# The pooled branch's products as one sum of three 256-column passes, and a later place for two weight loads

## The chip, the cores and the metric

The kernel runs on one core of a Trainium2 chip. The metric is the device time of one execution in microseconds; less is better. A core has a matmul engine (TensorE, PE in the profile, its weight loads PEld), VectorE (DVE), ScalarE (ACT), GpSimd (POOL) and SyncE (SP), whose queue issues nearly all DMA transfers here. Each engine runs its own instructions in order and waits on the others by semaphores. Matmuls read SBUF and write PSUM, which has eight banks of 128 x 512 float32; four of them (`mmp`, tag `mm`) serve the sums that this change is about.

## What is computed

An encoder trunk of two layers over 256 tokens of 1024 channels, in float32. A layer has a token mixer (a pooled branch, an attention branch, gates and an output projection) and a gated MLP with a convolution of width 3. Of the reference, cut to the pooled branch and the MLP:

```python
pooled = jnp.stack([_centred_mean(ug[:, :, gi], w) for gi, w in enumerate(POOL_WINDOWS)], axis=2) - ug
pool_out = jnp.einsum('bsgc,gcd->bsgd', pooled, w_pool).reshape(B, S, POOL_WIDTH) * pool_scale
...
merged = jax.nn.sigmoid(g_pool) * (pool_out @ w_a) + jax.nn.sigmoid(g_attn) * (attn_out @ w_b)
...
a, gval = jnp.split(xn @ w_up, 2, axis=-1)
a = lax.conv_general_dilated(a, conv_w[:, None, :], ...) + conv_b
return (jax.nn.gelu(a) * gval) @ w_down
```

There are four pooled groups of 256 channels each, so `w_pool` has four products of 256 tokens by 256 channels by 256 channels in a layer.

## The kernel before

**Two parts for every operand.** TensorE works on a 32-bit type with fewer mantissa bits than float32. Every weight and every activation is therefore split into a high part, rounded to that type, and a rest: `wh` and `wl`, `x2[..., 0]` and `x2[..., 1]`. A product is the sum of high by high, high by rest and rest by high. The split of a weight piece (128 x 1024 numbers) is one ScalarE copy (L252) and one VectorE subtraction (L254).

**The stream of weights.** The class `Weights` holds two lists that are written down before the kernel starts: `loads` (transfers of 1 MB from memory into a raw tile, issued on SP's queue by L171) and `pieces` (halves of a load, or slices, in the order in which TensorE uses them). `W.get()` hands out the next piece and makes sure that the three or four behind it are being split. A raw tile is one of three (`RAW`); the next load waits until both of its pieces are split. A split piece is one of five (`BUFS`); ScalarE waits until TensorE has left it. Loads leave in the order in which they were added. A load with a tag of its own (`ybig`, `at2`) goes into another tile and doesn't count among the three.

**The mixer and the pooled branch.** The input projection runs in groups (`GROUPS`) of 512 columns; each is four steps of 12 matmuls (L753, tile `t_ps`, 512 columns each). Between the steps of the last two groups, q1 and k1, stand the pooled branch's products, one of the four groups behind every second step: `visits` lists which generator is advanced behind which step. `pool_out` works a group off in two stages that are separated by a `yield`, so that the second stage is issued one step later. A group has two chunks of 128 output channels. For a chunk, `two_sums` multiplies the high weight by both parts of the pooled values at once (512 columns), and the weight's rest by the high part (256 columns, into the second half of the bank). ScalarE then scales the second half (L1166), VectorE scales the first and adds (L1169); one step later ScalarE rounds the result to `po2`'s high part (L1175) and VectorE subtracts it (L1178). `po2` is used from the second half of the next projection on.

**The MLP.** `MLP_GROUPS` sets the order: g0, a1, g1, a2, g2 (groups of the up projection, 512 columns in four steps; a0 ran before), then `("w", 3)`, a block that makes two further groups out of seven products of quadrants of the weight instead of eight, with steps of the down projection (tile `res_ps`, L670 to L672) between them. The block's products are L1582. Two of its quadrants, "11" and "12", are loaded by `first_quadrants` into the tiles tagged `ybig` and `at2` ahead of the block, because their differences (L343) are weights as well. When a group's sums are complete, VectorE transposes them (L807), one transfer of 0.5 MB sends them to memory (L812, tile `crossing`), and four transfers bring them back with channels on the partitions (L819, tiles `zga` and `zg`). All of these share SP's queue with the loads.

Of the kernel before, what the change touches and what calls it, by code (L numbers as in the profile page):

```python
# [289 lines left out]
def encoder(ctx, tc, x, w_in, w_pool, pool_scale, w_a, w_b, w_o, norm1, norm2, w_up, conv_w,  # L290
            conv_b, w_down, rel_bias, norm_f, onehot, edges, out):
    nc = tc.nc
# [71 lines left out]
    for l in range(DEPTH):  # L364
        for g in range(NG):
            c0 = C_V + g * 512
            slots = (("m2", 0, 2), ("m2", 1, 2), ("ybig",), ("at2",)) if g == 0 else ()
            for j in range(2):
                tag = "k1" if l == 0 and g == 1 and j == 0 else None
                W.use(rows(w_in[l], j * 512, 4, c0, 512, tag), slots[2 * j : 2 * j + 2])  # L370
        if l == 0:
            W.n_scaled = len(W.pieces)
        for kind, n in GROUPS:
            c0 = {"u": 0, "q": C_Q, "k": C_K}[kind] + n * 512
            pieces = rows(w_in[l], 0, 4, c0, 512)
# [84 lines left out]
    hps = const.tile([P, DEPTH, 8], F32, name="hps")  # L460
# [178 lines left out]
            nc.sync.dma_start(out=ov[:, t, middle], in_=xn[:, middle])  # L639
            yield  # L640

    turns = {"rest": False}

    def two_sums(x2, nk, *chunks):

        wide, rests = ([(c, k, kind) for c in chunks for k in range(nk)] for kind in (True, False))
        first = rests if turns["rest"] else wide
        last = wide if turns["rest"] else rests
        for steps in (first, last):
            for (ps, wh, wl), k, kind in steps:
                out, w, x = (ps, wh, x2[:, k]) if kind else (ps[:, 1], wl, x2[:, k, 0])
                nc.tensor.matmul(  # L657
                    out, w(k), x, start=(steps is first and k == 0),
                    stop=(steps is last and k == nk - 1), skip_group_check=turns["rest"],
                )  # L660
        turns["rest"] = not turns["rest"]

    def halves(a):

        return a.rearrange("p (t m) -> p t m", t=2)
# [360 lines left out]
    for l in range(DEPTH):  # L1026
# [21 lines left out]
        if l == 0:  # L1048
            with tc.manual_schedule():
                begun = begin_values_of_x()  # L1050
                W.by_hand = 1
                x2 = first_values(*begun, keep_values)
                W.by_hand = 0
        else:
            for g in range(NG):
                held = begun[0] if g == 0 else [W.get() for _ in range(4)]
                for t in range(2):
                    if g + t == 0:
                        ps = begun[1]
                    else:  # L1060
                        ps = v_tile()
# [34 lines left out]
        us, pooled, got = {}, {}, {}  # L1096
# [50 lines left out]
        def pool_out():  # L1147
            for j in (1, 0):
                if j:
                    po2 = got["po2"] = two_parts("m2", "po2")  # L1150
                i, (wh, wl) = W.get()
                for gg in range(2):
                    ps = [mmp.tile([P, 2, S], F32, tag="mm", name="pool_ps") for _ in range(2)]
                    for oc in range(2):
                        cc = slice(oc * P, (oc + 1) * P)
                        two_sums(
                            pooled[2 * j + gg], 2,
                            (ps[oc], lambda k: wh[:, 2 * gg + k, cc], lambda k: wl[:, 2 * gg + k, cc]),
                        )
                    if gg:  # L1160
                        W.free(i)
                    po = [sm.tile([P, 2, P], F32, tag="u", name="po") for _ in range(2)]
                    first = 4 * j + 2 * gg
                    for oc in range(2):
                        sc = hps[:, l, first + oc : first + oc + 1]
                        nc.scalar.mul(out=po[oc], in_=halves(ps[oc][:, 1]), mul=sc)  # L1166
                    for oc in range(2):
                        sc = hps[:, l, first + oc : first + oc + 1]
                        nc.vector.scalar_tensor_tensor(  # L1169
                            out=po[oc], in0=halves(ps[oc][:, 0]), scalar=sc, in1=po[oc],  # L1170
                            op0=ALU.mult, op1=ALU.add,
                        )
                    yield
                    for oc in range(2):
                        nc.scalar.copy(out=po2[:, first + oc, 0], in_=po[oc])  # L1175
                    for oc in range(2):
                        c = first + oc
                        nc.vector.tensor_sub(out=po2[:, c, 1], in0=po[oc], in1=po2[:, c, 0].bitcast(F32))  # L1178
                    yield

        first_parts = {}
# [119 lines left out]
        def keep_gated(n):  # L1301
# [36 lines left out]
        with tc.manual_schedule():  # L1338
            W.by_hand = 1
            for kind, n in GROUPS:  # L1340
                ps = None
                for i in range(4):
                    ps = by_tokens(x2, 4, ps=ps, begin=i, end=i + 1)
# [6 lines left out]
            po2 = got["po2"]  # L1350
# [15 lines left out]
            first = None  # L1366
# [314 lines left out]
```

## Time and profile before

| | us |
|---|---|
| median of 3 runs | 850.63 |
| lowest, highest | 850.13, 852.48 |
| the profiled execution | 851.33 |
| its span, from the first instruction to the last | 849.5 |
| TensorE busy | 840.6 |
| VectorE busy | 645.6 |
| ScalarE busy | 523.8 |

The profile is of one execution. Its span is what the views show; the 1.8 us between the span and the execution's time lie before and behind. Matmuls overlap in the pipeline, so a matmul's duration (0.39 us for 512 columns) is longer than its share of the time: what counts is the step from one start to the next. A row of the timeline has start, duration, engine, line, operation, tiles, shapes and count, and in brackets how long the engine had been idle and what ended it.

### The profile page before, as it was taken

What the parts mean: (1) busy time and instruction counts of PE and PEld (TensorE: products, weight loads), DVE (VectorE), ACT (ScalarE), POOL (GpSimd) and SP (SyncE); (2) the same over time, 40 slices, a digit from 0 to 9 for tenths busy, and PEclk for the clock granted to TensorE, in tenths of its full rate; (3) what the DMA queues carried; (4) which work ended last, traced back from release to release, by engine and by line L of the source; (5) the groups of instructions that cost most, each with busy time, mean ns of one, the idle gap of its engine ahead of it and who ended that gap; (6) DMA issues with size and microseconds to landing.
All of it is one profiled execution on the core that took longest, in us unless ns stands there. A gap on an engine that the chain in (4) does not pass through costs nothing.

```text
span 849.5 us, 10951 instructions
## 1 busy us (share of the span) xinstructions
PE 840.6 (99%) x3901; PEld 700.9 (83%) x3901; DVE 645.6 (76%) x838; ACT 523.8 (62%) x757; POOL 34.0 (4%) x96
## 2 busy tenths in 40 slices
PE   9999999999999999999999999999999999999997
PEld 7888888888888878888888888888888888888886
DVE  6968777757767699898665686878567878998874
ACT  7744566654554776688645454677455658757883
POOL 1610000000010000000000000000000100000000
PEclk9999999999999999999999999999999999999999
DMA  8699897785759885898735889868777499769861
GB/s 303 213 307 294 302 292 242 260 276 210 251 191 299 278 266 198 264 328 294 232 120 200 261 275 313 279 206 271 252 250 278 152 332 296 246 205 289 305 198 51
DMA packets 147968, 214.03 MB, mean 252 GB/s; under 512 B 7801, under 2 KB 69185, under 8 KB 147913
## 3 DMA queue, kind: packets, MB, share of 16 engines
q1 hardware_dynamic: 147480, 212.67, 75.9%
q10 hardware_dynamic: 432, 0.66, 0.2%
q8 instruction: 31, 0.51, 0.2%
q14 instruction: 25, 0.20, 0.1%
HBM read 186.02 MB, written 27.28 MB: 251 GB/s over the span
## 4 chain that ended last, share of the span: by engine, by line
PE 89%; DMA 4%; DVE 4%; ACT 1%; issue 1%; SPq 0%; POOL 0%; ACTq 0%; DVEq 0%; POOLq 0%
PE t_ps L753 53%; PE res_ps L670 6%; PE res_ps L671 6%; PE res_ps L672 6%; PE v_ps L753 6%; PE t_ps L1582 4%; PE v_ps L1006 3%; DMA raw<-in_w_up_dram 2%; DVE wl L254 1%; PE pool_ps L657 1%; PE v_ps L905 1%; DMA crossing<-crossing 1%; PE o_ps L1289 1%; PE s_ps L1241 1%; PE s_ps L1236 1%; PE o_ps L1285 1%
## 5 line engine op out<-in xcount | busy, mean ns | idle before, releaser
L254 DVE TENSOR_TENSOR wl<-raw,wh 128x1024 fp32r<-128x1024 f32 x286 | 344.1, 1217 | 114.9 <-ACT wh L252 113.2
L252 ACT CAST wh<-raw 128x1024 fp32r<-128x1024 f32 x286 | 296.9, 1049 | 170.2 <-PE t_ps L753 86.2
L753 PE MATMUL t_ps<-wh,x 128*128 128x512 f32 x1280 | 399.8, 390 | 0.0
L753 PEld LDWEIGHTS t_ps<-wh,x 128*128 128x128 f32 x1280 | 240.3, 188 | 49.8
L753 PE MATMUL t_ps<-wl,x 128*128 128x512 f32 x640 | 249.0, 389 | 0.0
L753 PEld LDWEIGHTS t_ps<-wl,x 128*128 128x128 f32 x640 | 120.2, 188 | 25.0
L671 PE MATMUL res_ps<-wl,actq 128*128 128x512 f32 (+1 forms) x184 | 69.9, 380 | 0.2 <-DVE wl L254 0.2
L670 PE MATMUL res_ps<-wh,actq 128*128 128x512 f32 (+1 forms) x184 | 70.0, 380 | 0.0
L672 PE MATMUL res_ps<-wh,actk 128*128 128x512 f32 (+1 forms) x184 | 69.3, 380 | 0.0
L753 PE MATMUL t_ps<-wh,po 128*128 128x512 f32 x128 | 41.4, 395 | 0.0
L671 PEld LDWEIGHTS res_ps<-wl,actq 128*128 128x128 f32 x184 | 34.6, 188 | 7.3 <-DVE wl L254 0.7
L672 PEld LDWEIGHTS res_ps<-wh,actk 128*128 128x128 f32 x184 | 34.6, 188 | 6.6
L670 PEld LDWEIGHTS res_ps<-wh,actq 128*128 128x128 f32 x184 | 34.6, 188 | 6.5
L1492 ACT ACTIVATE a<-zga,prm 128x256 f32<-128x256 f32 x80 | 38.9, 513 | 0.0
L547 POOL TENSOR_SCALAR ss<-ss 128x1 f32<-128x1 f32 x8 | 2.1, 266 | 767.8 <-ACT junk L540 767.8
L753 PEld LDWEIGHTS t_ps<-wh,po 128*128 128x128 f32 x128 | 24.0, 188 | 4.9
L670 PE MATMUL res_ps<-wh,m 128*128 128x512 f32 (+1 forms) x72 | 26.5, 368 | 0.0
L671 PE MATMUL res_ps<-wl,m 128*128 128x512 f32 (+1 forms) x72 | 26.3, 365 | 0.0
L540 ACT ACTIVATE junk<-h 128x512 f32<-128x512 f32 (+1 forms) x19 | 10.5, 554 | 25.2 <-DVE h L562 25.0
L672 PE MATMUL res_ps<-wh,m 128*128 128x512 f32 (+1 forms) x72 | 26.0, 366 | 0.0
L1496 DVE TENSOR_TENSOR y<-y,a 128x510 f32<-128x510 f32 x22 | 14.9, 679 | 14.1 <-ACT y L1490 14.1
L753 PE MATMUL v_ps<-wh,x 128*128 128x512 f32 x80 | 25.7, 392 | 0.0
(211 smaller groups left out, 1067.2 us busy)
## 6 DMA issues: line engine op xcount, KB each, us to landing
raw<-in_w_in_dram SPq DMA_DIRECT2D x58, 1024.0 KB
raw<-in_w_up_dram SPq DMA_DIRECT2D x40, 1024.0 KB
raw<-in_w_down_dram SPq DMA_DIRECT2D x22, 1024.0 KB
crossing<-crossing SPq DMA_DIRECT2D x22, 512.0 KB
crossing<-way SPq DMA_DIRECT2D x16, 512.0 KB
raw<-in_w_a_dram SPq DMA_DIRECT2D x8, 1024.0 KB
raw<-in_w_o_dram SPq DMA_DIRECT2D x8, 1024.0 KB
zga<-crossing SPq DMA_DIRECT2D x40, 128.0 KB
```

The source lines that it names most:

```text
L252: inst = nc.scalar.copy(out=h, in_=src)
L254: inst = self.rests[i] = nc.vector.tensor_sub(out=l, in0=src, in1=h.bitcast(F32))
L540: nc.scalar.activation(junk[:, 0 : cc.stop - cc.start], h[:, t, cc], AF.Square, scale=D**-0.5, accum_out=ss[:, n : n + 1],)
L657: nc.tensor.matmul(out, w(k), x, start=(steps is first and k == 0), stop=(steps is last and k == nk - 1), skip_group_check=turns["rest"],)
L670: nc.tensor.matmul(ps, ah, wh, start=first, stop=False, skip_group_check=on)
L671: nc.tensor.matmul(ps, ah, wl, start=False, stop=False, skip_group_check=on)
L672: nc.tensor.matmul(ps, al, wh, start=False, stop=last, skip_group_check=on)
L753: nc.tensor.matmul(ps, x2[:, 2 * n + j, part, t, :], w[:, j, :], start=(n + m == 0), stop=(n == last and m == 5),)
L1006: nc.tensor.matmul(ps[t], a[:, k, t, :], w[:, j, :], start=(k + m == 0), stop=(k == KD - 1 and m == 2),)
L1492: nc.scalar.mul(out=out, in_=a, mul=row(j, c))
L1496: nc.vector.tensor_add(out=y[:, :, 1:], in0=y[:, :, 1:], in1=t["a0"][:, :, : S - 1])
L1582: nc.tensor.matmul(ps, operands[name](part, 2 * j + c), w[:, c, :], start=(name in opens and j + m == 0), stop=(j == 1 and m == 5), skip_g ...
```

## The change

There are two edits. The first makes the pooled branch's products in another way: for each chunk six matmuls of 256 columns, three passes for each of two halves of the contraction, add into one half bank. ScalarE writes `po2`'s high part from the bank, scaled, in one instruction; one step later VectorE writes the rest in one instruction, from the same bank. The tile `po` and the second stage's copy and subtraction are gone. The second edit adds the loads of the quadrants "11" and "12" to the list ahead of g2's loads instead of ahead of a2's.

```diff
-            if (kind, n) == ("a", 2):
+            if (kind, n) == ("g", 2):
                 corner = first_quadrants(w_up[l], 3)
...
-    def two_sums(x2, nk, *chunks):
-        wide, rests = ([(c, k, kind) for c in chunks for k in range(nk)] for kind in (True, False))
-        first = rests if turns["rest"] else wide
-        last = wide if turns["rest"] else rests
-        for steps in (first, last):
-            for (ps, wh, wl), k, kind in steps:
-                out, w, x = (ps, wh, x2[:, k]) if kind else (ps[:, 1], wl, x2[:, k, 0])
-                nc.tensor.matmul(
-                    out, w(k), x, start=(steps is first and k == 0),
-                    stop=(steps is last and k == nk - 1), skip_group_check=turns["rest"],
-                )
-        turns["rest"] = not turns["rest"]
+    def one_sum(x2, nk, ps, wh, wl, c):
+        cc = slice(c * P, (c + 1) * P)
+        passes = [(k, w, part) for k in range(nk) for w, part in ((wh, 0), (wl, 0), (wh, 1))]
+        for m, (k, w, part) in enumerate(passes):
+            nc.tensor.matmul(ps, w[:, k, cc], x2[:, k, part], start=(m == 0), stop=(m == 3 * nk - 1))
...
-                    po = [sm.tile([P, 2, P], F32, tag="u", name="po") for _ in range(2)]
                     first = 4 * j + 2 * gg
-                    for oc in range(2):
-                        sc = hps[:, l, first + oc : first + oc + 1]
-                        nc.scalar.mul(out=po[oc], in_=halves(ps[oc][:, 1]), mul=sc)
-                    for oc in range(2):
-                        sc = hps[:, l, first + oc : first + oc + 1]
+                    parts = [
+                        (hps[:, l, c : c + 1], halves(ps[c - first]), po2[:, c, 0], po2[:, c, 1])
+                        for c in (first, first + 1)
+                    ]
+                    for sc, p, hi, _ in parts:
+                        nc.scalar.mul(out=hi, in_=p, mul=sc)
+                    yield
+                    for sc, p, hi, lo in parts:
                         nc.vector.scalar_tensor_tensor(
-                            out=po[oc], in0=halves(ps[oc][:, 0]), scalar=sc, in1=po[oc],
-                            op0=ALU.mult, op1=ALU.add,
+                            out=lo, in0=p, scalar=sc, in1=hi.bitcast(F32), op0=ALU.mult, op1=ALU.subtract
                         )
-                    yield
-                    for oc in range(2):
-                        nc.scalar.copy(out=po2[:, first + oc, 0], in_=po[oc])
-                    for oc in range(2):
-                        c = first + oc
-                        nc.vector.tensor_sub(out=po2[:, c, 1], in0=po[oc], in1=po2[:, c, 0].bitcast(F32))
                     yield
```

SP's queue in layer 0, from the loads of a1 to those of g2, before. The numbers behind `raw` count tiles: 2434 and 2444 are a1's two loads, 2535 and 2537 the two quadrants, 2466 and 2500 g1's, 2539 and 2573 a2's, 2625 g2's first.

```order
L171 DMA raw_2434<-in_w_up_dram 128x4x512
L415 DMA gain<-in_norm_dram 128x1024
L171 DMA raw_2535<-in_w_up_dram 128x4x512
L171 DMA raw_2444<-in_w_up_dram 128x4x512
L812 DMA crossing<-crossing 128x2x512
L171 DMA raw_2537<-in_w_up_dram 128x4x512
L819 DMA zga<-crossing 32x8x128 x4
L171 DMA raw_2466<-in_w_up_dram 128x4x512
L171 DMA raw_2500<-in_w_up_dram 128x4x512
L812 DMA crossing<-crossing 128x2x512
L171 DMA raw_2539<-in_w_up_dram 128x4x512
```

The same queue with the change, from g1's second load on (2492). Line numbers are those of the changed file: L798 is the send that was L812, L805 the reads that were L819. 2527 and 2561 are a2's loads, 2613 and 2619 the quadrants, 2621 and 2658 g2's.

```order
L171 DMA raw_2492<-in_w_up_dram 128x4x512
L798 DMA crossing<-crossing 128x2x512
L171 DMA raw_2527<-in_w_up_dram 128x4x512
L805 DMA zg<-crossing 32x8x128 x4
L171 DMA raw_2561<-in_w_up_dram 128x4x512
L798 DMA crossing<-crossing 128x2x512
L171 DMA raw_2613<-in_w_up_dram 128x4x512
L805 DMA zga<-crossing 32x8x128 x4
L171 DMA raw_2619<-in_w_up_dram 128x4x512
L171 DMA raw_2621<-in_w_up_dram 128x4x512
L171 DMA raw_2658<-in_w_up_dram 128x4x512
```

The two quadrants move past two sends, the eight reads behind them and all four loads of g1 and a2; they now lie around the third reads, with g2's loads right behind them.

VectorE in layer 0 at the pooled branch's second and third groups, before: the transposes of q1's sums, the two passes of a pooled group, and the weight splits between them.

```order
L807 STREAM_TRANSPOSE way<-t_ps 128x4x4x32 x2
L1169 SCALAR_TENSOR_TENSOR po<-pool_ps,hps,po 128x256 x2
L254 TENSOR_TENSOR wl_1204<-raw_1047,wh_1203 128x1024
L254 TENSOR_TENSOR wl_1208<-raw_1047,wh_1207 128x1024
L1178 TENSOR_TENSOR po_1126<-po,po_1126 128x256 x2
L254 TENSOR_TENSOR wl_1228<-raw_1108,wh_1227 128x1024
```

The same place with the change (L793 is L807, L1153 the new pass):

```order
L793 STREAM_TRANSPOSE way<-t_ps 128x4x4x32 x2
L254 TENSOR_TENSOR wl_1202<-raw_1047,wh_1201 128x1024
L254 TENSOR_TENSOR wl_1206<-raw_1047,wh_1205 128x1024
L1153 SCALAR_TENSOR_TENSOR po_1126<-pool_ps,hps,po_1126 128x256 x2
L254 TENSOR_TENSOR wl_1224<-raw_1108,wh_1223 128x1024
```

The pass that reads the bank `pool_ps` now stands behind two weight splits, where the second of the two old passes stood; the next pooled products use the same bank.

More of the change, by code (lines that the diff above doesn't have):

```diff
@@ L640, in finish @@
             yield
-    turns = {"rest": False}
-    def two_sums(x2, nk, *chunks):
-        wide, rests = ([(c, k, kind) for c in chunks for k in range(nk)] for kind in (True, False))
-        first = rests if turns["rest"] else wide
-        last = wide if turns["rest"] else rests
-        for steps in (first, last):
-            for (ps, wh, wl), k, kind in steps:
-                out, w, x = (ps, wh, x2[:, k]) if kind else (ps[:, 1], wl, x2[:, k, 0])
-                nc.tensor.matmul(
-                    out, w(k), x, start=(steps is first and k == 0),
-                    stop=(steps is last and k == nk - 1), skip_group_check=turns["rest"],
-                )
-        turns["rest"] = not turns["rest"]
+    def one_sum(x2, nk, ps, wh, wl, c):
[3 more added lines that the diff above has]
+            nc.tensor.matmul(ps, w[:, k, cc], x2[:, k, part], start=(m == 0), stop=(m == 3 * nk - 1))
     def halves(a):
@@ L1152, in pool_out @@
                 for gg in range(2):
-                    ps = [mmp.tile([P, 2, S], F32, tag="mm", name="pool_ps") for _ in range(2)]
+                    ps = [mmp.tile([P, S], F32, tag="mm", name="pool_ps") for _ in range(2)]
                     for oc in range(2):
[L1155 to L1159, printed above, removed]
+                        one_sum(pooled[2 * j + gg], 2, ps[oc], wh[:, 2 * gg :], wl[:, 2 * gg :], oc)
                     if gg:
                         W.free(i)
-                    po = [sm.tile([P, 2, P], F32, tag="u", name="po") for _ in range(2)]
                     first = 4 * j + 2 * gg
-                    for oc in range(2):
-                        sc = hps[:, l, first + oc : first + oc + 1]
-                        nc.scalar.mul(out=po[oc], in_=halves(ps[oc][:, 1]), mul=sc)
-                    for oc in range(2):
-                        sc = hps[:, l, first + oc : first + oc + 1]
+                    parts = [
[6 more added lines that the diff above has]
+                    for sc, p, hi, lo in parts:
                         nc.vector.scalar_tensor_tensor(
-                            out=po[oc], in0=halves(ps[oc][:, 0]), scalar=sc, in1=po[oc],
-                            op0=ALU.mult, op1=ALU.add,
-                        )
-                    yield
-                    for oc in range(2):
-                        nc.scalar.copy(out=po2[:, first + oc, 0], in_=po[oc])
-                    for oc in range(2):
-                        c = first + oc
-                        nc.vector.tensor_sub(out=po2[:, c, 1], in0=po[oc], in1=po2[:, c, 0].bitcast(F32))
+                            out=lo, in0=p, scalar=sc, in1=hi.bitcast(F32), op0=ALU.mult, op1=ALU.subtract
+                        )
                     yield
```

## Prediction

> **What bounds the kernel now.** I read the page first, then the waits of TensorE, then the timeline where TensorE waits, then back along ScalarE, VectorE and the load queue to what started that wait.
>
> ```profile
> PE 840.6 (99%) x3901; PEld 700.9 (83%) x3901; DVE 645.6 (76%) x838; ACT 523.8 (62%) x757; POOL 34.0 (4%) x96
> PEclk9999999999999999999999999999999999999999
> ```
>
> TensorE is busy in 840.6 of 849.5 us, at full clock in every slice. Whatever is taken from VectorE or ScalarE counts only where TensorE waits for it, and the list of TensorE's waits is short:
>
> ```profile
> PE t_ps L1582 <- DVE crossing L807: 0.9, 1, 0.9
> ...
> PE xt_ps L582 <- DVE xn L573: 0.3, 1, 0.3
> ```
>
> The second is a layer boundary that the change doesn't touch. The first lies in layer 0, at the start of the MLP's block, and its place in the timeline shows more than 0.9 us:
>
> ```profile
> 314.75 0.39 PE L670 MATMUL res_ps<-wh,actq 128*128 128x512 f32 x1
> 315.38 0.50 PE L671 MATMUL res_ps<-wl,actq 128*128 128x512 f32 x1 [0.25 <-DVE wl L254]
> 315.72 0.40 PE L672 MATMUL res_ps<-wh,actk 128*128 128x512 f32 x1
> ...
> 317.78 0.39 PE L672 MATMUL res_ps<-wh,actk 128*128 128x512 f32 x1
> 319.04 0.47 PE L1582 MATMUL t_ps<-wh,sx 128*128 128x512 f32 x1 [0.87 <-DVE crossing L807]
> ```
>
> Starts are to be read here, not durations. A 512-column matmul normally follows the last by 0.227 us (5.45 us for 24, in a row below). Here the steps are 0.63, 0.34 and 1.26 us: **0.40 + 0.11 + 1.03 = 1.54 us** lost, all of it waiting for split weights and for a transpose that stood late in VectorE's queue. Outside the first 10 us and the layer boundary this is the only stall of the execution, so 1.54 us is all that removing waits can bring. Why were VectorE and ScalarE late?
>
> ```profile
> ACT wh L252 <- DMA raw<-in_w_up_dram: 15.0, 4, 8.8
> ```
>
> ```profile
> 275.87 2.00 ACT L252 CAST wh<-raw 128x1024 fp32r<-128x1024 f32 x2 [8.78 <-DMA raw<-in_w_up_dram]
> ...
> 290.61 1.05 ACT L252 CAST wh<-raw 128x1024 fp32r<-128x1024 f32 x1 [3.56 <-DMA raw<-in_w_up_dram]
> ...
> 296.50 1.03 ACT L252 CAST wh<-raw 128x1024 fp32r<-128x1024 f32 x1
> ```
>
> ```profile
> 276.95 2.36 DVE L254 TENSOR_TENSOR wl<-raw,wh 128x1024 fp32r<-128x1024 f32 x2 [7.10 <-ACT wh L252]
> ...
> 291.69 1.23 DVE L254 TENSOR_TENSOR wl<-raw,wh 128x1024 fp32r<-128x1024 f32 x1 [2.78 <-ACT wh L252]
> ...
> 318.19 1.31 DVE L807 STREAM_TRANSPOSE crossing<-t_ps 128x512 f32<-128x512 f32 x2
> ```
>
> In the four groups before the block ScalarE waited 15.0 us for up-projection loads (between 255 and 322 us); VectorE waited behind it at 276.95 and 291.69, and its transposes of g2's sums, which had been ready at 312, came at 318.19. The loads were late because two of the block's quadrants went ahead of them:
>
> ```profile
> 255.10 2.44 SPq L171 DMA_DIRECT2D raw<-in_w_up_dram  x2
> ...
> 259.95 0.67 SPq L171 DMA_DIRECT2D raw<-in_w_up_dram  x1
> 266.08 1.81 SPq L819 DMA_DIRECT2D zga<-crossing  x4
> 267.99 0.94 SPq L171 DMA_DIRECT2D raw<-in_w_up_dram  x2
> ...
> 283.29 0.38 SPq L812 DMA_DIRECT2D crossing<-crossing  x1
> ```
>
> ```profile
> 259.53 6.53 DMA crossing<-crossing
> ...
> 307.52 3.61 DMA crossing<-crossing
> ```
>
> By the order of the queue the first issue at 255.10 and the one at 259.95 are the two quadrants, 1 MB each; g1's loads follow only at 267.99, since the reads at 266.08 waited 6.53 us for a transfer that takes 3.61 us at 307.52.
>
> **The quadrants' move.** Both quadrants now stand behind a2's loads and ahead of g2's. Take g0, a1, g1, a2, g2 as the groups: each is 16 x 2.72/4 = 10.88 us of TensorE, and counting back from the block's first matmul (12 matmuls before 314.75, so 312.03) g1 begins at 279.4, a2 at 290.3, g2 at 301.15.
>
> Without the quadrants the transfer of 259.53 takes some 3.6 us instead of 6.53, its reads go out at about 263, and g1's loads at 265 instead of 267.99, with nothing ahead of them but those reads. ScalarE has g1's first piece at 270 to 271 instead of 275.87, a2's second load no longer comes last, and the wait of 3.56 us at 290.61 goes too. What is late next is g2: its first load now stands behind both quadrants. They go out after the send of a1, which moves from 283.29 to about 281 (a1's sums end at 279.4, two transposes of 0.65 us). From there the queue holds quadrant, a send and its reads of 0.5 MB each, quadrant, g2's first load: 4.2 MB.
>
> ```profile
> 281.00:294.00 13.00, 13.00 (x59) 10.78 (x58) 8.31 (x10) 9.41 (x17) 0.00 (x0) 1.00 0.81 262
> ...
> 301.00:308.00 7.00, 7.00 (x33) 5.79 (x32) 7.00 (x8) 4.92 (x9) 0.00 (x0) 1.00 1.02 328
> ```
>
> The last two columns are the share in which the DMA engines were busy and GB/s. At the full rate of 328 the 4.2 MB take 13 us, and 2 us pass between issue and landing beside the bytes (3.61 us for 0.5 MB at 307.52): g2's first load lands near 296, against 296.50 when ScalarE took that piece before, and its second 3.3 us later, at 299.3 instead of a piece taken at 300.4. From there to the transposes VectorE has the same work back to back, so these come 0.5 to 1.5 us earlier. I take **-1.1 us in layer 0**; the ends are 0 (the wait only moves) and -1.54 (all of it). Layer 1 has the same order, no stall, and something to lose:
>
> ```profile
> 711.99 1.04 ACT L252 CAST wh<-raw 128x1024 fp32r<-128x1024 f32 x1
> ...
> 718.12 1.05 ACT L252 CAST wh<-raw 128x1024 fp32r<-128x1024 f32 x1 [0.69 <-PE t_ps L753]
> ```
>
> ```profile
> 731.68 2.72 PE t_ps L1582 x12
> ```
>
> ```profile
> 735.34 0.38 SPq L812 DMA_DIRECT2D crossing<-crossing  x1
> ```
>
> It runs 419.5 us behind layer 0, so 711.99 is 292.5 in layer 0's times: g2's first piece was taken 4 us earlier there than in layer 0, and by 718.12 ScalarE was waiting for TensorE again. The transposes ended before 735.34, the first of the two about 734.7; TensorE needed it two stretches of 2.72 us after 731.68, at 737.1. That is 2.4 us to spare, and g2's second load comes some 2.5 us later than before: **+0.15 us in layer 1**, between 0 and 2.
>
> **The pooled products.** 32 matmuls of 512 columns and 32 of 256 become 96 of 256; the columns are the same, the weight loads 96 instead of 64.
>
> ```profile
> L657 PE MATMUL pool_ps<-pl,wh x32: 389/392/398, 111.7 to 552.9; 128*128 128x512 f32 x32
> ```
>
> ```profile
> 111.84 1.40 PE pool_ps L657 x8
> 113.23 5.45 PE t_ps L753 x24
> ...
> 144.66 0.35 PE s_ps L1236 x3
> ...
> 242.52 0.12 PE res_ps L670
> ```
>
> Before, 8 groups of 1.395 us make 11.16 us. 256-column matmuls with weights of their own take 0.117 us (0.35 for three) to 0.12 us. At 0.118 the 96 take 11.33 us: **+0.17 us**. The ends are half of 0.227 (10.90, so -0.26) and 0.12 (11.52, so +0.36). The Trainium skill's page "TensorE: Matmul & The Clock Gate" (section "Wait — 56ns, not 53.3ns?") has matmuls follow each other by columns over 2.4 GHz plus some 2.5 ns; by it 32 more matmuls would add 0.08 us. This trace has 0.227 us where that rule gives 0.216, so the fixed part is larger here, and the row stands.
>
> Of the sixteen chunks each loses one of two ScalarE and one of two VectorE instructions. TensorE waited for none of them, so this is worth nothing in itself. What it costs is cover: VectorE's only pass now reads the bank one step later, and the next group of products waits for it.
>
> ```profile
> 121.56 2.36 DVE L254 TENSOR_TENSOR wl<-raw,wh 128x1024 fp32r<-128x1024 f32 x2 [0.46 <-ACT wh L252]
> 123.84 0.75 DVE L1178 TENSOR_TENSOR po<-po,po 128x256 fp32r<-128x256 f32 x2
> ```
>
> ```profile
> 125.37 0.62 PE L657 MATMUL pool_ps<-pl,wh 128*128 128x512 f32 x2
> ```
>
> ```profile
> L1169 DVE SCALAR_TENSOR_TENSOR po<-pool_ps,hps,po x16: 474/481/485, 114.2 to 553.8; 128x256 f32<-128x256 f32 x16
> ```
>
> At the tightest of the three places in a layer the new pass stands where L1178 did, behind the same two splits: the first ends at 123.84 + 0.48 = 124.3, and TensorE wants its bank at 125.37. One microsecond is left, so 0. Were VectorE one split (1.2 us) later, TensorE would wait 0.2 us there; that is the price without cover.
>
> **Sum.** The profiled execution took 851.33 us, a span of 849.5 and 1.8 around it. 851.33 - 1.1 + 0.15 + 0.17 = **850.5 us**. The median shown is 850.63; the three runs (850.13 to 852.48) differ by more than the stall, which hangs on how fast the transfers happen to be, so I take nothing off again.
>
> **Rivals.** *The wait only moves.* g2's first load lands at 297 instead of 296, VectorE ends as late as before: 851.33 + 0.17 = 851.5. For it: 4.2 MB stand ahead of that load. Against: layer 1, with g2's piece 4 us earlier, has no stall at all.
>
> *Slower: the quadrants hold g2 back.* The queue moves them first; if transfers run at under some 300 GB/s there (262 in the row of 281 to 294, where the engines were idle a fifth of the time), g2's first load lands after 297. At 298 layer 0 loses 1.5 us more than now and layer 1, where the piece was taken at 292.5, some 2 us: 851.33 + 0.17 + 1.5 + 2 = 855.0. The Trainium skill's "DMA: Bandwidth & Descriptors" (section "Queues, rings and completion order") has each DMA engine consume descriptors in ring order, which speaks for this rival and against the change; the 6.53 us at 259.53 agree with it.
>
> *Banks held too long.* If VectorE is later than in this trace at the pooled places, TensorE waits some 0.3 us at three places in each of two layers: 850.5 + 1.8 = 852.3. Against: a microsecond is left at the tightest.
>
> *All goes well.* The stall goes whole, layer 1 keeps its lead, 256 columns cost 0.1135: 851.33 - 1.54 - 0.26 = 849.5.
>
> **Numbers.** Chances: forecast 0.55, the wait only moves 0.18, slower 0.10, banks 0.07, all goes well 0.10. The range from 849.3 to 852.8 holds all but the slower rival, with what the unknown costs make of the others. A measurement of this kernel can tell about 0.3% (2.55 us) from no change. Only a part of the slower rival lies above 853.2: slower 0.09. Faster by as much needs more than the whole stall: 0.03. Within: 0.88.
>
> **What would show it.** Right: no step over 0.3 us between TensorE's starts at the block of layer 0, ScalarE's waits for up-projection loads well under 15.0 us and moved from g1 to g2, 96 pooled matmuls about 0.118 us apart, and no wait of TensorE on the pooled pass. Wrong: a wait of TensorE for g2's weights in either layer, a stall of the same length at the block's start, or pooled products waiting for VectorE.

## The result, and the profile after

| us | before | changed |
|---|---|---|
| median of 7 runs each, on one chip | 850.63 | 853.10 |
| lowest, highest | 849.77, 852.48 | 852.59, 856.25 |
| the profiled execution, its span | 851.33, 849.5 | 852.59, 850.7 |

The changed kernel takes 1.0034 of the time before, with a 95% interval from 1.0019 to 1.0049. That is 2.5 us slower and 0.3 us above the upper end of the predicted range, whose most likely time was 850.5.

The list of TensorE's waits in the changed kernel (engine, tile and line waiting, whom for: total, times, longest). Lines moved up by 14 to 23: L1582 is L1559 now, L807 is L793, L670 to L672 are L656 to L658.

```profile
PE t_ps L1559 <- DVE crossing L793: 1.1, 2, 0.9
...
PE res_ps L657 <- DVE wl L254: 0.3, 1, 0.3
```

The stall that was to go is still there, and the first line now counts two places instead of one. TensorE's timeline at the block, first layer 0, then layer 1:

```profile
315.09 0.39 PE L656 MATMUL res_ps<-wh,actq 128*128 128x512 f32 x1
315.75 0.50 PE L657 MATMUL res_ps<-wl,actq 128*128 128x512 f32 x1 [0.28 <-DVE wl L254]
316.09 0.40 PE L658 MATMUL res_ps<-wh,actk 128*128 128x512 f32 x1
...
318.18 0.39 PE L658 MATMUL res_ps<-wh,actk 128*128 128x512 f32 x1
319.42 0.47 PE L1559 MATMUL t_ps<-wh,sx 128*128 128x512 f32 x1 [0.85 <-DVE crossing L793]
```

```profile
737.32 0.39 PE L658 MATMUL res_ps<-wh,actk 128*128 128x512 f32 x1
737.99 0.47 PE L1559 MATMUL t_ps<-wh,sx 128*128 128x512 f32 x1 [0.28 <-DVE crossing L793]
```

Starts against the usual step of 0.227 us: in layer 0 0.44 + 0.11 + 1.01 = 1.56 us are lost (before: 1.54), and in layer 1, which had no stall, 0.44. ScalarE's waits between 255 and 322 us and its timeline say what happened on the way:

```profile
ACT wh L252 <- DMA raw<-in_w_up_dram: 10.2, 2, 6.4
```

```profile
271.26 2.00 ACT L252 CAST wh<-raw 128x1024 fp32r<-128x1024 f32 x2 [3.82 <-DMA raw<-in_w_up_dram]
...
298.03 1.05 ACT L252 CAST wh<-raw 128x1024 fp32r<-128x1024 f32 x1 [6.39 <-DMA raw<-in_w_up_dram]
```

The first half of the change's effect came as predicted: g1's pieces are taken at 271.26 instead of 275.87, and the wait for them fell from 8.78 to 3.82 us. But a wait of 6.39 us now stands ahead of g2's first piece, which is taken at 298.03, where the forecast had 296 and the kernel before 296.50. In layer 1 the same piece came at 716.61, where it was 711.99.

**Where the bytes went.** The load of the DMA engines in four stretches shows why. The last two columns are the share in which the DMA engines were busy and GB/s; 257 to 268 and 676 to 687 are the stretches that the quadrants left, 281 to 298 and 700 to 717 those into which they moved. Before:

```profile
257.00:268.00 11.00, 11.00 (x50) 9.13 (x49) 11.00 (x13) 6.45 (x7) 0.00 (x0) 1.00 0.99 333
281.00:298.00 17.00, 17.00 (x77) 14.08 (x76) 11.77 (x15) 12.71 (x21) 0.00 (x0) 1.00 0.86 272
676.00:687.00 11.00, 11.00 (x50) 9.13 (x49) 11.00 (x13) 6.94 (x7) 0.00 (x0) 1.00 0.94 343
700.00:717.00 17.00, 17.00 (x76) 14.08 (x75) 13.62 (x17) 13.30 (x20) 0.00 (x0) 1.00 0.94 297
```

Changed:

```profile
257.00:268.00 11.00, 11.00 (x50) 9.09 (x50) 11.00 (x13) 6.79 (x7) 0.00 (x0) 1.00 0.63 199
281.00:298.00 17.00, 17.00 (x77) 14.08 (x76) 10.03 (x13) 9.55 (x14) 0.00 (x0) 1.00 1.01 327
676.00:687.00 11.00, 11.00 (x51) 9.09 (x49) 11.00 (x13) 7.34 (x8) 0.00 (x0) 1.00 0.61 195
700.00:717.00 17.00, 17.00 (x77) 14.08 (x76) 10.76 (x14) 10.67 (x17) 0.00 (x0) 1.00 1.04 348
```

The early stretch was full and is now a third empty: 11 us at 333 - 199 = 134 GB/s are 1.5 MB that no other transfer took the place of. SP's queue in that stretch shows why none did:

```profile
259.87 0.37 SPq L798 DMA_DIRECT2D crossing<-crossing  x1
264.10 1.81 SPq L805 DMA_DIRECT2D zga<-crossing  x4
266.01 1.14 SPq L171 DMA_DIRECT2D raw<-in_w_up_dram  x2
```

g1's loads stand behind four reads that wait for the send issued at 259.87 to land. For 4.2 us the queue issues nothing, and the DMA engines run dry at the end of it: from 264 to 268 they moved 154 GB/s at a share of 0.61 (before: 372 at 0.98). A second gap lies ahead of the send: from 257 to 260 they moved 74 GB/s at a share of 0.33 (before: 359 at 1.01), since the queue's first load of this stretch went out at 257.51, where before the first quadrant went out at 255.10. The quadrants had filled both gaps. The late stretch was nearly full and is now entirely full: 17 us x 327 GB/s = 5.6 MB, at the highest rate seen there, and still g2's load is late.

**The pooled products.** The 12 matmuls of a pooled group in the changed kernel, with the first matmul behind the next part of the mixer in the second fence:

```profile
111.83 0.28 PE L647 MATMUL pool_ps<-pl,wh 128*128 128x256 f32 x1
111.94 0.28 PE L647 MATMUL pool_ps<-pl,wl 128*128 128x256 f32 x1
112.06 0.40 PE L647 MATMUL pool_ps<-pl,wh 128*128 128x256 f32 x2
112.30 0.28 PE L647 MATMUL pool_ps<-pl,wl 128*128 128x256 f32 x1
```

```profile
144.87 0.52 PE L1213 MATMUL s_ps<-khl,qhl 128*128 128x256 f32 x3
```

Steps are 0.12 us. From the first pooled product to the attention's first score it was 144.50 - 111.68 = 32.82 us before, start to start, and is 144.87 - 111.83 = 33.04 now: 0.22 us more in a layer, 0.44 in both (layer 1 has the same steps). TensorE waits nowhere for the pooled passes.

Between the two profiled executions the span grew by 1.2 us: 0.46 of stalls, 0.44 of pooled products, and 0.3 that is spread over steps without a gap of its own. The changed kernel's profiled execution was the fastest of its seven, though, so most of its others lost more; a second profile of it, below, lost 5.1 us in stalls.

### The profile page after: what moved, and what is told of

It is laid out like the page before. It is cut to its first block, busy times and chain, and to the rows that moved or that the text cites. A ratio compares the mean times of both kernels' runs of the same rounds, so it can differ in the third digit from the quotient of the medians.

```text
span 850.7 us, 10995 instructions
## 1 busy us (share of the span) xinstructions
PE 842.1 (99%) x3933; PEld 703.5 (83%) x3933; DVE 638.5 (75%) x822; ACT 517.4 (61%) x741; POOL 35.1 (4%) x96
## 4 chain that ended last, share of the span: by engine, by line
PE 85%; DVE 6%; DMA 5%; ACT 2%; issue 1%; SPq 0%; POOL 0%; DVEq 0%; ACTq 0%; POOLq 0%
PE t_ps L739 48%; PE res_ps L656 6%; PE res_ps L657 6%; PE res_ps L658 6%; PE v_ps L739 6%; PE t_ps L1559 4%; PE v_ps L992 3%; DMA raw<-in_w_up_dram 2%; DVE wl L254 2%; DMA crossing<-crossing 2%; PE v_ps L891 1%; PE pool_ps L647 1%; DVE crossing L793 1%; PE o_ps L1266 1%; PE s_ps L1218 1%
## 5 line engine op out<-in xcount | busy, mean ns | idle before, releaser
L656 PE MATMUL res_ps<-wh,actq 128*128 128x512 f32 (+1 forms) x184 | 70.0, 380 | 0.0
L658 PE MATMUL res_ps<-wh,actk 128*128 128x512 f32 (+1 forms) x184 | 69.3, 380 | 0.0
L656 PEld LDWEIGHTS res_ps<-wh,actq 128*128 128x128 f32 x184 | 34.6, 188 | 6.6
L658 PEld LDWEIGHTS res_ps<-wh,actk 128*128 128x128 f32 x184 | 34.6, 188 | 6.6
L656 PE MATMUL res_ps<-wh,m 128*128 128x512 f32 (+1 forms) x72 | 26.5, 368 | 0.0
L658 PE MATMUL res_ps<-wh,m 128*128 128x512 f32 (+1 forms) x72 | 26.0, 365 | 0.0
```

What stands on the lines that cost most here:

```text
L656: nc.tensor.matmul(ps, ah, wh, start=first, stop=False, skip_group_check=on)
L658: nc.tensor.matmul(ps, al, wh, start=False, stop=last, skip_group_check=on)
```

## The experiments

Two theories stood against each other at first. **Bytes:** the quadrants' 2 MB make g2's first load late wherever they go ahead of it in that full stretch, and the loss is the stall that follows. **Pooled products:** narrow matmuls and the bank held longer cost the time, and the loads are neutral. Later it was also asked whether the order in SP's queue, rather than the bytes, holds g2 back.

In the times below the kernel before ran on the same chip: 849.79, 849.88 and 850.01 us in the three batches. Where a number is called "behind the marker", the marker is the first `xt_ps` matmul of the MLP in that layer (243.44 and 662.93 us in the kernel before).

### One part of the change at a time

The changed kernel once more:

> The changed kernel once more, beside its halves. Both theories: +2.0 to +2.8 us against before. If the halves add up, e1 and e2 together give this. Its profile is a second look at the changed kernel: theory L expects the stalls at the block to be longer than the 1.56 and 0.44 us of the first profile, which was of the fastest execution.

Measured: 854.42 us (851.77 to 856.80), 1.0050 [1.0032, 1.0068]. That is 4.4 us, more than the 2.0 to 2.8 that both theories expected; the stalls in its profile are longer than in the first one, as expected, 1.74 and 3.4 us.

The pooled products alone:

```diff
-            if (kind, n) == ("g", 2):
+            if (kind, n) == ("a", 2):
                 corner = first_quadrants(w_up[l], 3)
```

> The pooled products in one sum, the quadrants loaded where they were before. Theory L (the quadrants' new place makes most of the loss, since g2's first load lands behind them): +0.4 us against before, the 32 more matmuls alone, and layer 1 without a stall at the block. Theory P (the pooled edit makes most of it, in executions that the one profile of the change doesn't show): +1.5 to +2.5 us.

Measured: 850.61 us (850.14 to 852.78), 1.0010 [1.0002, 1.0019]. The only wait at the block in its profile:

```profile
PE t_ps L1559 <- DVE crossing L793: 0.3, 1, 0.3
```

The quadrants' move alone (the same edit the other way, in the kernel before):

> Only the quadrants' loads move, the pooled products as before. Theory L: +1.5 to +2.2 us against before; ScalarE waits 5 us or more for g2's first load in layer 0, and TensorE stalls at the block's start in both layers. Theory P: within 0.5 us of before.

Measured: 855.20 us (853.11 to 856.16), 1.0053 [1.0039, 1.0067]: 5.4 us over the median before, more than twice what was expected. Its layer 1, ScalarE and then TensorE:

```profile
717.98 1.06 ACT L252 CAST wh<-raw 128x1024 fp32r<-128x1024 f32 x1 [7.07 <-DMA raw<-in_w_up_dram]
```

```profile
734.26 0.40 PE L1582 MATMUL t_ps<-wh,x 128*128 128x512 f32 x1
735.53 0.50 PE L670 MATMUL res_ps<-wh,actq 128*128 128x512 f32 x1 [0.88 <-ACT wh L252]
736.86 0.50 PE L671 MATMUL res_ps<-wl,actq 128*128 128x512 f32 x1 [0.82 <-DVE wl L254]
```

What follows: the move of the two loads makes nearly all of the loss, 3.3 to 5.7 us when done alone; the pooled products cost 0.8 us (0.2 to 1.6). In layer 1 g2's first piece was taken 7.07 us after ScalarE was free for it, and TensorE lost 1.05 + 1.10 us at the two starts shown, 3.8 us with the others around them. The two losses don't add up (the whole change was no slower than the move alone); the intervals are too wide to say whether that means anything.

### The narrow matmuls alone

In the kernel before, each 512-column pooled matmul is made as two of 256 with the same weight; the passes on ScalarE and VectorE stay as they were. The edit, shortened:

```diff
-                nc.tensor.matmul(out, w(k), x, ...)
+                for part in range(2) if kind else (None,):
+                    nc.tensor.matmul(out[:, part], w(k), x[:, part], ...)
```

> Before, but each pooled matmul of 512 columns is issued as two of 256 with the same weight; ScalarE's and VectorE's passes and the loads are those of before. 96 matmuls of 256 columns as in the changed kernel. If the narrower matmuls are all that the pooled edit costs: the same +0.3 to +0.8 us as the pooled edit alone, 12 steps of 0.12 us in each group. If the bank that is held one step longer costs too: less here than in the pooled edit alone, by a wait of TensorE.

Measured: 851.16 us (850.07 to 852.32), 1.0009 [0.9999, 1.0018], like the pooled part of the change, though its interval doesn't exclude that nothing changed. The profiles are finer: from the first pooled product to the first score it takes 33.04 us in each layer here, in the pooled products alone and in the changed kernel, and 32.82 or 32.83 in every run with the products of before. What follows: the extra 32 matmuls explain that part, some 0.4 us in both layers together; the fewer passes and the bank held longer show no gain and no loss beside it.

### Where the quadrants stand, and how many bytes they are

Both quadrants behind g2's loads:

```diff
-            if (kind, n) == ("a", 2):
+            if kind == "w":
                 corner = first_quadrants(w_up[l], 3)
```

> The quadrants' loads behind g2's instead of ahead of them, pooled products as before. Theory L: ScalarE no longer waits over 1 us for a load of g2; what is late now are the quadrants themselves, which stand behind the reads of zg (about 302 us in layer 0) and land near 306, while VectorE wants their difference (L343) at 303: it waits some 3 us in each layer, and the block's start stalls by 1 to 3 us in each layer: +1 to +5 us. If VectorE's and ScalarE's lead at g2 is what decides and not the quadrants, no stall at all: -1 us in layer 0, 0 in layer 1.

Measured: 857.41 us (857.17 to 858.11), 1.0090 [1.0076, 1.0105]. g2's pieces now come early, but the quadrants' differences, for which VectorE waits, come late:

```profile
305.04 1.23 DVE L343 TENSOR_TENSOR raw<-raw,raw 128x1024 f32<-128x1024 f32 x1 [6.76 <-DMA raw<-in_w_up_dram]
```

VectorE runs its work in order, so what stands behind that wait, g2's work among it, is late all the same. The wait is more than twice the 3 us expected, and the loss of 7.5 us lies above the expected +1 to +5; in the profiled execution 1.4 us of it come from TensorE's clock (last section).

One quadrant at each place:

```diff
             if (kind, n) == ("a", 2):
-                corner = first_quadrants(w_up[l], 3)
+                corner = {"12": quadrant(w_up[l], 3, 0, 0, "at2")}
+            if (kind, n) == ("g", 2):
+                corner["11"] = quadrant(w_up[l], 3, 0, 1, "ybig")
```

> Before, with quadrant 12 loaded ahead of a2's loads as it was and quadrant 11 ahead of g2's. If the time is set by which load stands behind the quadrants, 1 MB less is ahead of g1 and 1 MB less ahead of g2: g2's first load lands some 3 us earlier than in the changed kernel (near 294), g1's some 3 us earlier than before, and the stall of 1.5 us in layer 0 shrinks below 0.5: -1.0 us against before, no stall in layer 1. If the stall comes from VectorE's and ScalarE's own work in the block, whatever the loads do: within 0.3 us of before.

Measured: 854.58 us (854.10 to 854.99), 1.0051 [1.0039, 1.0063]: no stall in layer 0, 3.9 us in layer 1. Neither expectation came for the whole: what was expected of the bytes held in layer 0 alone, and the time is that of the changed kernel.

The quadrants at the new place, but on ScalarE's DMA queue instead of SP's:

```diff
-                    self.nc.sync.dma_start(out=t, in_=src)
+                    queue = self.nc.scalar if tag in ("ybig", "at2") else self.nc.sync
+                    queue.dma_start(out=t, in_=src)
```

> The quadrants' loads at their new place in the list, pooled products as before, but both are issued on ScalarE's DMA queue instead of SP's. Theory ring order (g2's loads are late because the quadrants stand ahead of them in one queue): g2's first load overtakes, ScalarE takes it 2 us or more earlier than with the loads alone moved, and the time falls to at most 1.5 us over before. Theory bytes (the DMA engines are full, and whoever shares them is late): g2's first piece within 1 us of where it was, and 3.5 us or more over before.

Measured: 854.23 us (850.74 to 858.39), 1.0052 [1.0033, 1.0070], stalls of 1.53 us in layer 0 and 1.88 in layer 1. What follows: the quadrants needn't stand in the queue of g2's loads to hold them back. The run doesn't show that the order within SP's queue is without effect: g2's loads still stood behind the four reads there, and these went out at 291.05 instead of 285.09, most likely because the send shared the DMA engines with the quadrants.

At the new place, but only the first half of each quadrant is loaded; GpSimd sets the other half to zero, so half of two quadrants' terms is left out of the result:

```diff
-                    self.nc.sync.dma_start(out=t, in_=src)
+                    if tag in ("ybig", "at2"):
+                        self.nc.gpsimd.memset(t[:, 2:4], 0.0)
+                        self.nc.sync.dma_start(out=t[:, 0:2], in_=src[:, 0:2])
+                    else:
+                        self.nc.sync.dma_start(out=t, in_=src)
```

> The quadrants' loads at their new place, pooled products as before, but only the first half of each quadrant is loaded (0.5 MB instead of 1 MB) and GpSimd writes zeros into the rest, so the MLP's block is computed with half of two quadrants missing. Theory L (the place costs because 2 MB stand ahead of g2's loads): g2's first piece is taken 2.5 to 3.5 us earlier than with the full loads, the stalls at the block are under 0.5 us in each layer, and the time is within 1 us of before, some 4 us under the run with the loads alone moved. Rival (the place costs by something else than its bytes: the reads of a1 that wait behind the first quadrant, the issues): still 3 us or more over before.

Measured: 849.93 us (849.52 to 852.46), 1.0004 [0.9995, 1.0012], no stall at the block in either layer. ScalarE's row for g2's first piece in layer 0, to be set beside 298.03 above:

```profile
294.34 1.05 ACT L256 CAST wh<-raw 128x1024 fp32r<-128x1024 f32 x1 [2.82 <-DMA raw<-in_w_up_dram]
```

1 MB less at the same place, and the piece is taken 3.7 us sooner; 1 MB at 327 GB/s takes 3.2. This is the run that shows the bytes at work: same place, same queue, same order, half the bytes, and the loss is gone, though g2's loads were issued no earlier (at 288.17, against the row of three issues from 286.99 in the changed kernel). What it takes away is 1 MB of the whole traffic, however; with that 1 MB put back at the old place the loss returns ("A version that was to beat both").

The same halves at the old place:

> The kernel before with only the first half of each quadrant loaded, at its old place (the other half is set to zeros by GpSimd, so half of two quadrants' products is left out of the result's sums): 1 MB less in the early stretch and nothing in the late one. Theory: g1's first piece is taken some 3 us earlier than in the kernel before, g2's first piece before 52.5 us behind the marker in layer 0, no stall at the block, so 0.9975 to 0.9995 (the 1.5 us stall gone, the rest as before). Rival (the stall in layer 0 has another cause than the bytes ahead of g1's loads): the stall of 1.5 us stays, 0.9995 to 1.0005.

Measured: 850.22 us (849.78 to 851.64), 1.0002 [0.9993, 1.0011], no stall. The expected gain of up to 0.25% did not come, though the stall went. So in most executions of the kernel before there was hardly a stall to take away (below).

### A version that was to beat both

First halves of both quadrants at the old place, second halves at the new one; everything is computed.

```diff
+            for t, part in self.second.pop(self.n_loaded, ()):
+                self.nc.sync.dma_start(out=t[:, 2:4], in_=part[:, 2:4])
...
-                    self.nc.sync.dma_start(out=t, in_=src)
+                    if tag in ("ybig", "at2"):
+                        self.nc.sync.dma_start(out=t[:, 0:2], in_=src[:, 0:2])
...
```

> The kernel before, with the first half of each quadrant (1 MB in all) loaded at its place, ahead of g1's loads, and the second halves (1 MB) at the changed kernel's place, ahead of g2's loads. Everything is computed. Theory (2 MB fit neither place: early they make g1's loads late, late they make g2's late, and half of them fits in both): DMA share of 257:268 between 0.63 and 0.99, ScalarE takes g2's first piece before 52.5 us behind the marker in both layers, so no stall over 0.3 us at the block in either layer, and the time is that of the half quadrants run or a little less: 0.997 to 1.0005 of the kernel before. Rival (whatever stands ahead of g2's loads costs by its bytes, with no threshold): half of the changed kernel's loss, +1.0 to +1.8 us, 1.0012 to 1.002. Second rival (both places are bad): stalls as before in layer 0 and 1 to 2 us in layer 1, 1.002 or more.

Measured: 853.63 us (852.93 to 856.14), 1.0041 [1.0025, 1.0056]. The first theory's expectation failed: stalls of 0.53 us in layer 0 and 3.1 in layer 1, whose first rows are

```profile
716.00 1.05 ACT L259 CAST wh<-raw 128x1024 fp32r<-128x1024 f32 x1 [1.90 <-DMA raw<-in_w_up_dram]
```

```profile
733.14 0.39 PE L1591 MATMUL t_ps<-wh,x 128*128 128x512 f32 x1
734.26 0.50 PE L679 MATMUL res_ps<-wh,actq 128*128 128x512 f32 x1 [0.74 <-ACT wh L259]
735.59 0.50 PE L680 MATMUL res_ps<-wl,actq 128*128 128x512 f32 x1 [0.83 <-DVE wl L261]
```

It behaves like one quadrant at each place: in these runs 1 MB in the late stretch is harmless only when nothing was added in the early one. Why that is so, no run takes apart.

### All profiles side by side

When ScalarE takes g2's first piece, in us behind the marker, and what TensorE then loses at its late starts in g2 and at the block (starts beyond the usual step), layer 0 / layer 1, one execution each:

| MB early, late | kernel | taken | stall |
|---|---|---|---|
| 2, 0 | before | 53.05 / 49.06 | 1.54 / 0 |
| 2, 0 | pooled products alone | 51.48 / 49.32 | 0.41 / 0 |
| 2, 0 | narrow matmuls alone | 50.22 / 50.67 | 0 / 0 |
| 1, 0 | half quadrants, old place | 49.47 / 51.41 | 0 / 0 |
| 0, 1 | half quadrants, new place | 50.65 / 50.85 | 0 / 0 |
| 1, 1 | halves at both places | 51.74 / 53.94 | 0.53 / 3.1 |
| 1, 1 | one quadrant at each | 51.89 / 56.53 | 0 / 3.9 |
| 0, 2 | changed | 54.22 / 53.09 | 1.56 / 0.44 |
| 0, 2 | changed, again | 53.88 / 56.10 | 1.74 / 3.4 |
| 0, 2 | the move alone | 52.99 / 55.37 | 0.98 / 3.8 |
| 0, 2 | on ScalarE's queue | 53.99 / 54.54 | 1.53 / 1.88 |
| 0, 0 ahead of g2 | behind g2's loads | 47.87 / 47.75 | other cause |

A piece taken by 51.41 us has no stall behind it; from 52.99 on there always is one. Means of the classes: with nothing ahead of g2 47.8; 2 MB early 50.6; 2 MB late 54.3. Against the first, g2's first piece is 2.8 us later with the quadrants early and 6.5 us later with them late. At 327 GB/s 2 MB take 6.4 us: by these times the late place pays the whole of it, and the early one less than half, as the gaps there take the rest.

That 6.5 and 6.4 agree so closely is in part luck, since the table has times of taking and not of landing. Where ScalarE had other work first (at 296.50 in the kernel before no wait stands ahead of the row), the load was already there. The trace also marks the landing of each load, in sixteen parts. By the last part, g2's first load lands at 46.5 with nothing ahead of it, at 49.3 with 2 MB early and at 54.2 with 2 MB late (means, behind the marker): 2.8 and 7.7 us later. Beside the bytes its place in the queue has changed. Before, it is issued right behind the send, at 283.71 and 700.97, ahead of the four reads that wait for that send; in the changed kernel it stands behind these reads, in the rows of three issues from 286.99 and 706.43. The half quadrants left it behind the reads and had no stall, so the lost place alone doesn't make the loss; its share beside full quadrants was not measured.

Single executions of one class differ by up to 4 us, so the halves can't be put in order finely; why the first early megabyte alone costs nearly as much as two (50.4 against 50.6) stays open. That nothing but the quadrants can fill the gaps was read from the queue, not tried.

## Why the prediction was wrong, step by step

**The quadrants' move, layer 0: -1.1 us, measured 0.** The first half held (g1's pieces at 271, transfers and reads earlier, ScalarE's waits down from 15.0 to 10.2 us). The step that failed is the landing of g2's first load: "4.2 MB", "at the full rate of 328", 13 us from 281, and 2 us more, near 296. It landed at 298.03; with the same 2 us its bytes were through at 296, and the window up to there in the changed kernel reads

```profile
281.00:296.00 15.00, 15.00 (x68) 12.43 (x67) 10.03 (x13) 9.55 (x14) 0.00 (x0) 1.00 1.00 316
```

The engines were busy throughout, so 15 us x 316 GB/s = 4.7 MB were moved, where the sum had 4.2 with the load itself: 0.5 MB more (1.6 us) at a slightly lower rate (0.5 us). The 0.5 MB are most likely in the main the end of a2's second load, issued at 277.29 behind four reads, which the sum took as done at 281: the marks of its landing run from 282.07 to 283.54. The "full rate" is no single number either: with the engines full, 246 GB/s were moved from 286 to 292, while the four reads were under way, and 399 from 292 to 298. And the sum set a landing (296) beside a time of taking (296.50): before, the load had landed by 294.99, so that even a landing at 296 would have been a later one.

**Layer 1: +0.15 us (0 to 2), measured 0.44, 3.4 and 3.8 us in three profiles, 1.9 on the other queue.** This term was mis-sized most, and it decides the sign. "2.4 us to spare, and g2's second load comes some 2.5 us later" took a delay over from layer 0's estimate; g2's first piece came 4.0 to 7.0 us later there than before.

**What both terms overlooked.** The sum asked what stands ahead of g2 after the move, and not what the quadrants' old place would be used for. It took a move of 2 MB as neutral in bytes; 1.5 of them left a stretch that nothing else used, and went into one that was at 272 and 297 GB/s already.

**The pooled products: +0.17 us (-0.26 to +0.36), measured +0.44 between the profiles, 0.8 us (0.2 to 1.6) in the times.** The mechanism was right and the size too small: the steps are 0.12 us throughout, the upper end of the two rows it was taken from. The rule of the Trainium skill's page "TensorE: Matmul & The Clock Gate" (section "Wait — 56ns, not 53.3ns?"), columns over 2.4 GHz plus some 2.5 ns, gives 0.109 us; the trace shows 0.12, so the row stands over the rule here.

**The bank held one step longer: 0, measured 0.** No wait of TensorE on that pass in any profile.

**The base of the sum.** It began at a profiled execution of 851.33 us with a stall of 1.54 us in it. Kernels without any stall ran 849.93 and 850.22 us against 849.88 and 850.01 for the kernel before, and its code at that place showed 0 and 0.41 us in two other profiles. So most executions of the kernel before hardly had the stall that was to be gained; the prediction had noticed that the runs differ by more than the stall, and subtracted 1.1 us of it all the same. With 0.8 us for the pooled products even a perfect move would have ended about where the kernel before is.

**The rivals.** "The wait only moves" is what layer 0 did. "Slower: the quadrants hold g2 back" is what layer 1 did, and what decides the median; it had 0.10. Its price was 1.5 us in layer 0, where nothing was lost (a stall of 1.56 against 1.54), and 2 in layer 1, where 0.44 to 3.8 were; its 855.0 is near the 854.42 of the second series, but by luck. Its condition was wrong as well: it was to decide below 300 GB/s, and it did so at 327 and 348. The rule it leaned on, that descriptors are consumed in ring order (the Trainium skill's "DMA: Bandwidth & Descriptors", section "Queues, rings and completion order"), isn't needed for the loss: with the quadrants on another queue it was the same.

## What to carry to other kernels

Before a load is moved, ask both stretches: how full is the new one (busy share and GB/s), and what would run in the old one instead. If whatever comes next is held up by a buffer or by a wait in the queue, the bytes leave a hole behind and are added whole to the place they go to, as the 2 MB were here. Look too at what the next load then stands behind in the queue. And a stall seen in one profiled execution should be held against the spread of the times first: here it was not in most executions.

## What the runs showed of the hardware that was not expected

With both quadrants behind g2's loads, TensorE's clock was cut in half after a short stretch in which it was half idle. Windows of 3 us of that run (busy times of PE, PEld, DVE, ACT, POOL, then granted clock, DMA share, GB/s) and TensorE's rows in them:

```profile
315.00:318.00 3.00, 1.31 (x5) 0.56 (x4) 2.90 (x4) 3.00 (x5) 0.00 (x0) 0.96 0.83 216
318.00:321.00 3.00, 3.00 (x8) 2.33 (x8) 3.00 (x5) 2.42 (x4) 0.00 (x0) 0.50 0.00 0
321.00:324.00 3.00, 3.00 (x14) 2.39 (x14) 3.00 (x5) 3.00 (x5) 0.00 (x0) 0.97 0.46 169
```

```profile
318.59 0.63 PE L670 MATMUL res_ps<-wh,actq 128*128 128x512 f32 x1
319.01 0.63 PE L671 MATMUL res_ps<-wl,actq 128*128 128x512 f32 x1
319.44 0.63 PE L672 MATMUL res_ps<-wh,actk 128*128 128x512 f32 x1
```

TensorE was busy for 1.31 of 3 us; then the granted clock was 0.50 for 3 us, and 512 columns took 0.427 us instead of 0.227. Seven such steps cost 1.4 us more than usual ones, as much again as the longest of the stalls ahead of them (1.03 and 1.11 us). A run with stalls of the same length kept its full clock; the move alone, in layer 1:

```profile
734.00:737.00 3.00, 1.30 (x5) 0.52 (x4) 2.71 (x4) 3.00 (x6) 0.00 (x0) 1.00 0.43 151
```

There TensorE was busy for 1.30 of 3 us, no longer than at 315, and the clock stayed at 1.00. So the busy share of such a stretch doesn't decide by itself whether the clock falls; what does is open.

The same steps stood at the very start of one execution, that of the narrow matmuls alone:

```profile
7.85 1.91 PE L907 MATMUL v_ps<-m,xuh 128*128 128x512 f32 x4
9.56 0.81 PE L858 MATMUL xt_ps<-ident,h 128*128 128x128 f32 x3
```

Four matmuls in 1.71 us are 0.427 each (the view of the granted clock says 1.00 there, so the steps alone tell), and with those ahead of them some 1.7 us were lost there: its span was 850.1 us without any stall at the block, where the half quadrants, also without one, had 848.0. The kernel's start, not its loads, can therefore be a second reason why single times differ by one or two us; one execution shows it.
